# Fillers that move every large tile to a multiple of 512 bytes, and warm-up matmuls in float32r at several offsets

## The chip, the cores and the metric

The kernel runs on one core of a Trainium2 chip. The metric is the device time of one execution in microseconds (us); lower is better. Profiled times count from the start of the span, which is the time from the first to the last instruction.

## The reference

One decoder block on x of 512 positions by 1024 channels, all in float32:

```python
p = x @ w_in + b_in                        # 1024 -> 7184 columns
a_u, a_v, q, k, v, r, a_low, g_a, g_b = split(p)
y_a = gelu(a_u) * (causal_W_s @ layer_norm(gelu(a_v)) + b_s)      # 128-position chunks, 8 groups
log_f = log_sigmoid(a_low @ w_gate2 + b_gate) / 16
o = gated_linear_attention(q, k, v, log_f)                        # 4 heads, chunked
y_b = rms_norm(o) * norm_g * silu(r)
m = sigmoid(g_a) * y_a + sigmoid(g_b) * y_b
h = layer_norm(alpha * x + m @ w_out)
out = layer_norm(alpha * h + relu(h @ w_ff1)**2 @ w_ff2)          # 1024 -> 4096 -> 1024
```

## The kernel before, in words

**Three passes for one product.** Each operand of a large product is split into a float32r part "hi" (a cast on ScalarE, L90) and a remainder "lo" (a subtraction on VectorE, L91). A product is then three float32r matmuls: hi by hi, hi by lo, lo by hi. Activations stand in `xh`/`xl` (later `mh`/`ml` for m, `oh`/`ol` for combinations of the hidden layer, `Fs` and again `xh`/`xl` at the end); weights are streamed from HBM in chunks of 128 x 1024 (`raw`) and split into `wh`/`wl`, in rings of seven tiles each.

**Groups of 24.** Nearly all of TensorE's work is in groups of 24 matmuls, eight (or twice four) slices of the contraction by three passes, into one PSUM tile of 128 x 512. Which operand is stationary (loaded as 128 columns) and which one moves (512 columns) differs by line:

- L271 `first`: weights stationary, `xh`/`xl` moving; 4 groups.
- L204 `ps`: a row product. The activation is stationary, the weights move; 16 groups with `xh`/`xl`, and 8 with `mh`/`ml` (the product with w_out).
- L608 `qk`, `u`, `ga`, `r`, `gb` (36 groups) and `f`, the hidden layer (28 groups): weights stationary, `xh`/`xl` moving. Four more blocks of `f` run as 8 groups with 256 moving columns.
- L898 `m`: the second feed-forward product in a scheme of seven products for eight; `oh`/`ol` stationary, the weights move; 21 groups, alternating with groups of `f`.
- L984 `f`: the last quarter of that product; `Fs` or `xh`/`xl` stationary, the weights move; 7 groups of 512 columns and 2 of 256.

That is 120 groups of 24 with 512 columns and 10 with 256. Smaller work (scores `sc` L478, `pm` L656, `po` L504 to L508, transposes) runs in plain float32, each matmul as two instructions. The order of TensorE's instructions is the order of the program; from the hidden layer on that holds for the other engines too, and before it a scheduler orders them.

**Warm-up.** At the start `WARM = 9` float32 matmuls of 128 x 128 on the constant tile `ones` (L238) run while x and the first weights arrive.

**Where tiles lie.** Pools are stacked from both ends of each partition's memory, `side="left"` from below and `side="right"` from above, and each tile's start is rounded up to 32 bytes. As the program is built, the small constants in front (`ident`, `ones`, `ones_r`, `cols_sb`, three scalars) end at byte 18400 of each partition, and the right side starts at byte 229344. Both are multiples of 512 plus 480. Large tiles are multiples of 512 bytes long, so nearly all start there too:

| tiles | start, remainder by 512 |
|---|---|
| `xh`, `xl`, `wh`, `wl`, `als`, `dt`, `kt`, `bufA`, `bufB`, `raw`, `Fs` | 480 |
| `mh`, `ml`, `oh`, `ol` (behind the 896 bytes of statistics in pool `lnp`) | 352 |
| `ones_r` | 192 |
| `w2s`, `a_sb`, `wst` | 32 |
| `AT`, `QI`, `KD` of the first pair of heads; of the second | 480; 0 |

Slices of these tiles that go into a matmul begin at multiples of 512 bytes within the tile, so every stationary and every moving operand has the remainder of its tile.

Of the kernel before, what the change touches and what calls it, by code (L numbers as in the profile page):

```python
# [8 lines left out]
F32 = mybir.dt.float32  # L9
F32R = mybir.dt.float32r  # L10
# [5 lines left out]
P = 128  # L16
# [21 lines left out]
PAIRS = 3  # L38
ORDER = (2, 6, 3, 7, 4, 1, 5)
LEVELS = (32, 8, 2)  # L40
WARM = 9
QT_BUFS = 2
DIFF_K = "vector"
DIFF_Q = "gpsimd"
# [5 lines left out]
def hybrid_block(  # L50
# [20 lines left out]
    nc = tc.nc  # L71
    ctx.enter_context(tc.manual_schedule(engines={mybir.EngineType.PE}))

    def pool(stack, name, **kw):
        kw.setdefault("bufs", 1)
        return stack.enter_context(tc.tile_pool(name=name, reuse_waits="tile", **kw))

    const = pool(ctx, "const", side="left")
    xpool = pool(ctx, "xpool", side="left")
    wpool = pool(ctx, "wpool", side="left", bufs=W_BUFS)  # L80
    rpool = pool(ctx, "rpool", side="right", bufs=RAW_BUFS)
# [72 lines left out]
    ones = const.tile([P, P], F32, name="ones")  # L154
# [56 lines left out]
    def w_tile(u0, k, e):  # L211
        return [
            c.rearrange("p (k e) -> p k e", k=2)[:, k % 2, e * P : (e + 1) * P]
            for c in chunks[u0 + k // 2]
        ]
# [18 lines left out]
        nc.sync.dma_start(xraw[:, k0:k1, :], xT[:, k0:k1, :])  # L234

    wu = ps_a.tile([P, 512], F32, name="wu", tag="aux")
    for i in range(WARM):
        nc.tensor.matmul(wu[:, :P], ones, ones, start=True, stop=True)  # L238

    raw0 = rpool.tile([P, 1024], F32, name="raw0", tag="raw")  # L240
    raws[0] = [raw0]
# [9 lines left out]
    for k2 in range(KT // 2):  # L251
        split_to(k2 + 1)
        for k in (2 * k2, 2 * k2 + 1):
            wr = raw0[:, k * 512 : (k + 1) * 512] if k < 2 else None
            if k < 2:
                ksl = slice(k * 512, (k + 1) * 512)
                wh, wl = chunks[0]
# [10 lines left out]
            for i, e in order:  # L268
                wh, wl = w_tile(u0, k, e)
# [477 lines left out]
    lnp = pool(tail, "lnp", side="left")  # L747
    st1 = [lnp.tile([P, 2, 6], F32, name=f"st1_{t}") for t in range(NT)]
    st2 = [lnp.tile([P, 3, 6], F32, name=f"st2_{t}") for t in range(NT)]
    first_ln = ExitStack()  # L750
    ln1p = pool(first_ln, "ln1p", side="right")
    g1 = row_bcast(ln1p, ln1_g, D, "g1")
# [371 lines left out]
```

## Time and profile before

| | |
|---|---|
| median of three runs | 779.58 us (779.45 to 781.87) |
| profiled execution | 778.91 us, of which the span is 777.0 us |
| matmul instructions | 3498, busy 755.5 us |
| VectorE, ScalarE, GpSimd busy | 491.3, 355.7, 68.1 us |
| moved by DMA | 85.15 MB, mean 110 GB/s |

Busy time of TensorE is not its work at full rate: a matmul's record overlaps the next one's. What a group of matmuls costs is read from the time between the starts of successive groups.

### The profile page before, as it was taken

The page shows a single profiled execution, that of the slowest core. Times are in us where ns is not written, and L with a number is a line of the kernel's source. Part 1 is how long each engine was busy: PE and PEld are TensorE (multiplying, and loading weights), DVE is VectorE, ACT ScalarE, POOL GpSimd, SP SyncE. Part 2 cuts the span into 40 slices and gives each one's busy share as a digit, 9 for nine tenths or more (in the row PEclk, how much of TensorE's full clock was granted, in tenths as well). Part 3 has the DMA queues.
Part 4 walks back from the last instruction along what each step waited for, and adds up shares of the span by engine and source line. Part 5 has one row for each costly group of instructions (what it writes and reads, how often), then busy time and mean ns, then how long its engine had stood idle before and what let it go on. Part 6 is the DMA issues. An engine that isn't in the chain of part 4 may idle for free.

```text
span 777.0 us, 8849 instructions
## 1 busy us (share of the span) xinstructions
PE 755.5 (97%) x3498; PEld 627.2 (81%) x3498; DVE 491.3 (63%) x584; ACT 355.7 (46%) x453; POOL 68.1 (9%) x87
## 2 busy tenths in 40 slices
PE   8998999989999989999999999999999999999996
PEld 6887788878888877888888987888888888888785
DVE  6569666658666532445447545774687568869955
ACT  5476864353246544454322444555554444454300
POOL 1015400004202211000001000000000000000011
PEclk9999999999999999999999999999999999999999
DMA  7723332200341231422232522444154414335111
GB/s 274 262 74 116 102 129 81 82 28 27 109 136 55 74 130 36 151 85 93 97 101 76 163 82 83 159 136 138 54 162 136 147 69 145 130 132 163 54 55 54
DMA packets 25609, 85.15 MB, mean 110 GB/s; under 512 B 3104, under 2 KB 3360, under 8 KB 25568
## 3 DMA queue, kind: packets, MB, share of 16 engines
q1 hardware_dynamic: 25568, 84.59, 32.9%
q8 instruction: 27, 0.44, 0.2%
q14 instruction: 14, 0.11, 0.1%
HBM read 82.48 MB, written 2.10 MB: 109 GB/s over the span
## 4 chain that ended last, share of the span: by engine, by line
PE 85%; DVE 6%; ACT 3%; issue 2%; DMA 1%; POOL 1%; SPq 0%; DVEq 0%; POOLq 0%
PE f L608 22%; PE m L898 14%; PE ps L204 13%; PE gb L608 6%; PE r L608 6%; PE f L984 5%; PE u L608 5%; PE ga L608 4%; PE qk L608 3%; PE first L271 2%; DVE wl L91 2%; PE sc L478 2%; DMA raw<-in_w_all 1%; ACT wh L90 1%; PE po L504 1%
## 5 line engine op out<-in xcount | busy, mean ns | idle before, releaser
L91 DVE TENSOR_TENSOR wl<-raw,wh 128x1024 fp32r<-128x1024 f32 x144 | 176.9, 1238 | 152.1 <-ACT wh L90 145.3
L90 ACT CAST wh<-raw 128x1024 fp32r<-128x1024 f32 x144 | 148.7, 1045 | 137.9 <-PE ps L204 34.4
L608 PE MATMUL f<-xh,wl 128*128 128x512 f32 (+1 forms) x288 | 105.5, 366 | 0.0
L608 PE MATMUL f<-xh,wh 128*128 128x512 f32 (+1 forms) x288 | 105.4, 366 | 0.0
L608 PE MATMUL f<-xl,wh 128*128 128x512 f32 (+1 forms) x288 | 105.4, 366 | 0.0
L898 PE MATMUL m<-wh,ol 128*128 128x512 f32 x168 | 66.4, 395 | 0.5 <-DVE ol L91 0.5
L898 PE MATMUL m<-wh,oh 128*128 128x512 f32 x168 | 66.6, 396 | 0.3 <-ACT oh L90 0.3
L898 PE MATMUL m<-wl,oh 128*128 128x512 f32 x168 | 66.3, 395 | 0.0
L608 PEld LDWEIGHTS f<-xh,wh 128*128 128x128 f32 x288 | 54.3, 189 | 9.0
L608 PEld LDWEIGHTS f<-xl,wh 128*128 128x128 f32 x288 | 54.3, 189 | 9.0
L608 PEld LDWEIGHTS f<-xh,wl 128*128 128x128 f32 x288 | 54.3, 189 | 8.8
L204 PE MATMUL ps<-wh,xh 128*128 128x512 f32 x128 | 50.8, 397 | 0.0
L204 PE MATMUL ps<-wh,xl 128*128 128x512 f32 x128 | 49.9, 390 | 0.0
L204 PE MATMUL ps<-wl,xh 128*128 128x512 f32 x128 | 49.8, 389 | 0.0
L827 ACT ACTIVATE F<-f 128x512 f32<-128x512 f32 (+1 forms) x28 | 15.0, 537 | 75.9 <-PE f L608 75.9
L124 DVE TENSOR_TENSOR raw<-raw,raw 128x1024 f32<-128x1024 f32 x30 | 36.7, 1222 | 7.2 <-DMA raw<-in_w_all 6.9
L419 POOL TENSOR_TENSOR qt<-cum 128x768 f32<-128x768 f32 (+2 forms) x18 | 30.2, 1707 | 115.8 <-DVE cum L374 102.3
L898 PEld LDWEIGHTS m<-wh,ol 128*128 128x128 f32 x168 | 31.6, 188 | 8.4 <-DVE ol L91 1.0
L898 PEld LDWEIGHTS m<-wh,oh 128*128 128x128 f32 x168 | 31.6, 188 | 8.0 <-ACT oh L90 0.7
L898 PEld LDWEIGHTS m<-wl,oh 128*128 128x128 f32 x168 | 31.7, 189 | 7.4
L991 POOL TENSOR_TENSOR rs_l<-rs_l,nhalf 128x1 f32<-128x1 f32 x4 | 3.9, 986 | 332.9 <-DVE rs_l L990 332.9
L90 ACT CAST oh<-d 128x1024 fp32r<-128x1024 f32 x15 | 15.8, 1051 | 37.4 <-DVE d L824 37.4
(226 smaller groups left out, 1520.8 us busy)
## 6 DMA issues: line engine op xcount, KB each, us to landing
raw<-in_w_all SPq DMA_DIRECT2D x139, 512.0 KB, 3.3
xr<-in_x SPq DMA_DIRECT2D x8, 256.0 KB, 4.1
out<-bufA SPq DMA_DIRECT2D x8, 256.0 KB, 2.0
bufA<-in_xT SPq DMA_DIRECT2D x3, 512.0 KB, 9.0
brow<-in_b_in SPq DMA_DIRECT2D x4, 256.0 KB, 5.7
g<-in_ln_g SPq DMA_DIRECT2D x2, 512.0 KB, 4.6
b<-in_ln_b SPq DMA_DIRECT2D x2, 512.0 KB, 5.4
bufA<-in_xT SPq DMA_DIRECT2D x2, 256.0 KB, 3.3
```

Of the source, the lines that this page charges most:

```text
L90: nc.scalar.copy(hi, src)
L91: nc.vector.tensor_tensor(lo, src, hi.bitcast(F32), op=ALU.subtract)
L124: nc.vector.tensor_tensor(raw, raw, other[0], op=ALU.add if STREAM[i][0] == "sum" else ALU.subtract)
L204: nc.tensor.matmul(ps, s_, m_, start=(k == 0 and i == 0), stop=(k == KT - 1 and i == 2))
L271: nc.tensor.matmul(first[e], s_, m_[:, k, :], start=(k == 0 and i == 0), stop=(k == KT - 1 and i == 2))
L419: getattr(nc, DIFF_Q).tensor_tensor(qv[:, :, s0 : s0 + n, :], c4[:, :, d:4, :], c4[:, :, 0:n, h - 1 : h].broadcast_to([P, na, n, h]), op=A ...
L478: nc.tensor.matmul(sc[:, c, 0:192], pr.kt[:, jc * P : (jc + 1) * P], pr.qt[:, jc, :], start=True, stop=True)
L504: nc.tensor.matmul(po, pr.AT[:, j, c, :], vs, start=True, stop=(c == 0))
L608: nc.tensor.matmul(ps, s_, m_, start=(k == 0 and i == 0), stop=(k == KT - 1 and i == 2))
L827: nc.scalar.activation(dst, ps, AF.Relu)
L898: nc.tensor.matmul(ps, s_, m_, start=(k == 0 and i == 0), stop=(k == 3 and i == 2))
L984: nc.tensor.matmul(ps, s_, m_, start=(f == 0 and i == 0), stop=(f == 7 and i == 2))
```

## The change

Three tiles that nobody reads are added: 32 bytes behind the left side's constants (`pad_l`), 480 bytes at the right end (`pad_r`), 128 bytes behind the statistics of pool `lnp` (`pad_n`). The left side's large tiles then start at 18432 = 36 x 512, the right side's stack at 228864 = 447 x 512, and `mh`, `ml`, `oh`, `ol` at a multiple of 512 as well. All tiles that stood at remainder 480 or 352 stand at 0; `ones_r` stays at 192; `w2s`, `a_sb`, `wst` go to 64, and the second pair's `AT`, `QI`, `KD` from 0 to 32.

The nine float32 warm-up matmuls of 128 columns become 15 float32r matmuls of 512 columns. They read a tile `idle`, which takes the first place in the ring `wh`, is set to ones by VectorE (768 columns), and is read as the moving operand from 128 + o columns on, with o = 0, 4, 8, 24 and 40 columns (0, 16, 32, 96 and 160 bytes).

```diff
-WARM = 9
+WARM = (0, 0, 4, 4, 4, 8, 8, 8, 24, 24, 24, 40, 40, 40, 0)
...
     const = pool(ctx, "const", side="left")
+    const.tile([P, 8], F32, name="pad_l")
+    pool(ctx, "end", side="right").tile([P, 120], F32, name="pad_r")
     xpool = pool(ctx, "xpool", side="left")
...
-    for i in range(WARM):
-        nc.tensor.matmul(wu[:, :P], ones, ones, start=True, stop=True)
+    idle = wpool.tile([P, 1024], F32R, name="idle", tag="wh")
+    nc.vector.memset(idle[:, 0:768].bitcast(F32), 1.0)
+    for o in WARM:
+        nc.tensor.matmul(wu, idle[:, 0:P], idle[:, P + o : P + 512 + o], start=True, stop=True)
...
     st2 = [lnp.tile([P, 3, 6], F32, name=f"st2_{t}") for t in range(NT)]
+    lnp.tile([P, 32], F32, name="pad_n")
```

## Rows read from the trace of the kernel before

**Rows 1.** The page: busy time by engine, granted clock by slice, ending chain by engine.

```profile
PE 755.5 (97%) x3498; PEld 627.2 (81%) x3498; DVE 491.3 (63%) x584; ACT 355.7 (46%) x453; POOL 68.1 (9%) x87
...
PEclk9999999999999999999999999999999999999999
...
PE 85%; DVE 6%; ACT 3%; issue 2%; DMA 1%; POOL 1%; SPq 0%; DVEq 0%; POOLq 0%
```

**Rows 2.** Waits of TensorE, first and last of 13: total us, times, longest.

```profile
PE po L504 <- DVE t L714: 3.1, 2, 2.0
...
PE po L504 <- ACT bufB L522: 0.3, 1, 0.3
```

**Rows 3.** Chain that ended last, in order of time: start us, us, what.

```profile
33.51 10.88 PE ps L204 x48
...
103.41 1.30 PE sc L478 x8
...
382.43 33.47 PE ps L204 x144
...
428.82 2.87 PE f L608 x24
...
493.27 5.59 PE m L898 x24
498.86 5.46 PE f L608 x24
504.32 5.59 PE m L898 x24
509.90 5.46 PE f L608 x24
```

**Rows 4.** TensorE's groups by form: count | busy us, mean ns of one.

```profile
L608 PE MATMUL f<-xh,wl 128*128 128x512 f32 x224 | 87.3, 390 | 0.0
...
L898 PE MATMUL m<-wh,oh 128*128 128x512 f32 x168 | 66.6, 396 | 0.3 <-ACT oh L90 0.3
```

**Rows 5.** Windows: length, busy PE, PEld, DVE, ACT, POOL, clock, DMA share.

```profile
382.00:424.00 42.00, 42.00 (x190) 34.23 (x189) 25.06 (x32) 8.62 (x11) 2.65 (x4) 1.00 0.29 94
...
488.00:493.00 5.00, 5.00 (x24) 4.11 (x23) 3.68 (x5) 1.70 (x3) 0.00 (x0) 1.00 0.34 114
493.00:498.00 5.00, 5.00 (x24) 4.03 (x23) 3.59 (x4) 3.63 (x5) 0.00 (x0) 1.00 0.32 104
```

**Rows 6.** Timeline of the opening: start us, us, engine, line, instruction.

```profile
1.07 4.21 PE L238 MATMUL wu<-ones 128*128 128x128 f32 x18 [1.07 <-POOL bal L290]
...
4.70 1.84 DVE L259 CAST wh<-raw 128x512 fp32r<-128x512 f32 x1 [4.70 <-DMA raw<-in_w_all]
...
6.69 1.17 PE L271 MATMUL first<-xh,wh 128*128 128x512 f32 x4 [1.41 <-DVE wh L259]
...
8.60 1.07 PE L271 MATMUL first<-xh,wl 128*128 128x512 f32 x4
...
17.60 0.91 DVE L283 MEMSET als<- 128x1024 f32 x1 [0.16 <-issue]
```

**Rows 7.** The same chain in its first 30 us.

```profile
3.12 8.19 DMA raw<-in_w_all
...
12.42 1.24 DVE wl L91
...
13.70 16.18 PE first L271 x70
```

**Rows 8.** Timeline of TensorE around 165 us.

```profile
163.97 0.63 PE L608 MATMUL qk<-xl,wh 128*128 128x512 f32 x1
164.40 0.63 PE L608 MATMUL qk<-xh,wl 128*128 128x512 f32 x1
...
166.48 0.40 PE L608 MATMUL qk<-xl,wh 128*128 128x512 f32 x1
166.71 0.40 PE L608 MATMUL qk<-xh,wl 128*128 128x512 f32 x1
```

## The prediction

> **What bounds the kernel now.** I read the page first: TensorE is busy for 97% of the span, at full granted clock in every slice, and has 85% of the chain that ended last; VectorE is at 63% and ScalarE at 46% [rows 1]. Then TensorE's waits: the longest in total is 3.1 us, the last of the 13 is 0.3 us [rows 2], and the page's own chain leaves only 15% of the time to everything else. So the time is set by how closely matmuls follow each other, and that is read from the chain in order of time, as the distance of successive groups [rows 3]. The reader should see three numbers in it. A group of 24 with remainder 480 for both operands takes 10.88 / 2 = 5.44 us (L204 with `xh`, 48 matmuls) or 5.46 us (L608 `f` between two groups of `m`): 227 ns for each matmul. A group of `m`, with its stationary operand at remainder 352, takes 5.59 us, 233 ns each, and so do the groups with `mh`/`ml`: 33.47 us for 144, 5.58 us for 24 [rows 3]. And 512 columns at 2.4 GHz need 213.3 ns, so the fast kind pays 13.4 ns and the slow kind 19.6 ns on top of every matmul.
>
> **What the distance depends on.** The extra of the fast kind is a fixed piece: 256 columns take 2.87 us / 24 = 119.6 ns, that is 106.7 + 12.9 [rows 3]. It is hidden when the array takes its columns more slowly: at half the clock two matmuls start 0.43 us apart, which is 512 / 1.2 = 427 ns and nothing more, and 0.23 us apart just after [rows 8]; and a float32 score matmul, whose 192 columns take 1.30 us / 8 = 162.5 ns, that is 384 cycles or 160 ns and 2.5 [rows 3]. I conclude that the extra lies on the reading side, which keeps up with the array at full clock with little to spare. The extra of the slow kind goes with the place of the stationary operand: L204 is slow with `mh` and fast with `xh`, with the same weights moving. It does not go with ScalarE's load, which differs between `m` and `f` (3.63 against 1.70 us in 5 us) but is low in the stretch of `mh` too (8.62 in 42 us, 1.0 in 5) [rows 5].
>
> **The fillers, part one: the slow groups.** With `pad_n`, `mh`, `ml`, `oh` and `ol` get the remainder of the weights that move past them, as `xh` has it now. There are 21 groups of `m` (504 matmuls; the rows show a third of them, 168, for one pass [rows 4]) and 8 with `mh`/`ml`. If the distance follows the remainder of the stationary operand relative to the moving one, they fall to 5.45 us, the middle of 5.44 and 5.46: 21 x (5.59 - 5.45) + 8 x (5.58 - 5.45) = 2.9 + 1.0 = 3.9 us. A lower bound is 0 (the place is not the cause); I take 3.9, because the same line shows both distances.
>
> **Part two: the 13.4 ns of every matmul.** No matmul of the trace with 512 float32r columns has its moving operand at remainder 0, so its price is bounded by rows. Above: 5.59 us for a group, the worst that a remainder does here. Below: the extra falls to the 2.5 ns of the score matmul, 215.8 ns or 5.18 us for a group. The nearest row is the one with both operands at one remainder, 5.44 to 5.46; after the change both still share one. I take no change of the 13.4 ns and keep both ends.
>
> **The warm-up.** Removed: 18 instructions of 4.21 us, from 1.07 to 5.28 us [rows 6]. Added: a memset of 768 columns on VectorE, 768 / 1024 x 0.91 = 0.68 us, on an engine whose first other work starts at 4.70 us [rows 6], so it costs nothing there; and 15 matmuls of 512 columns, at half clock 0.427 us each [rows 8]. If VectorE starts about when GpSimd's constants are made, they begin near 1.6 us and, if all are at half clock, end at 1.6 + 15 x 0.427 = 8.0 us; if the clock rises where it rose before (the first real matmuls, from 6.69 us on, are 0.23 us apart), some three of them are fast and they end near 7.4. The first real matmul starts at 6.69 us, so it is late by 0.7 to 1.3 us. What hides that: the chain of this stretch runs over the second chunk of weights (DMA to 11.31, `wl` from 12.42, TensorE goes on at 13.70) [rows 7]. Before 13.70 TensorE has 26 real matmuls, 26 x 0.227 = 5.9 us in a stretch of 7.0, so 1.1 us of lateness is absorbed. Cost: 0 to 0.2 us; I take 0. Uncovered, it would be the 1.3 us, and if the clock rose late enough for 12 real matmuls at 0.427, some 2.4 us more. `idle` takes one place in the ring of `wh`; seven tiles later `wh5` takes its place, and the warm-up is then long over, while `wh6` reuses the place of `wh0` as before. No transfer moves.
>
> **Rest.** The float32 matmuls change their places too, but they have the reading to spare (2.5 ns over their columns [rows 3]): 0. `ones_r` stays off by 192 for 16 matmuls: 0. VectorE and ScalarE keep their operations: 0. The stretch near 165 us, where the clock was at half for six to seven matmuls [rows 8], costs 6.5 x 0.2 = 1.3 us now; it hangs on a wait and may go or come again: plus or minus 1.3.
>
> **Sum.** 778.91 - 3.9 = 775.0 us for an execution like the profiled one. The median of the runs is 0.67 us above that one, so 775.7 us, with 772 to 778 as this case's own range.
>
> **The rivals.**
> *A. The 13.4 ns go too.* 32 columns of 4 bytes at 2.4 GHz are 13.3 ns, and remainder 480 is 32 bytes short of a boundary; a read that begins inside a 128-byte piece touches one piece more, for 256 columns as for 512, and a slower array hides it. All three fit. Against it: a fixed cost of each load of a stationary operand fits as well. Price: 91 groups x (5.45 - 5.18) + 29 x (5.59 - 5.18) + 10 x (2.87 - 24 x 0.1092) = 24.6 + 11.9 + 2.5 = 39 us at most; as 85% of the chain is TensorE's [rows 1], I count 33: 779.6 - 33 = 746 us (741 to 768, since part of the extra may stay). [...]
> *B. Nothing changes.* The slow groups are slow for another reason than the place, say the side on which the weights are written while they move; then 779.6 us, 777.4 to 782. For it: `m` and the `mh` groups are also late in the kernel. Against it: the `f` between the `m` are as late and take 5.46 us [rows 3]. [...]
> *C. Slower.* With every operand at the same boundary, the load of the next stationary operand and the moving stream, which start together, meet in the same place at every matmul, and all groups take what the worst take now: 91 x (5.59 - 5.45) + 10 x 0.06 = 13 us, 779.6 + 13 = 793 us at the worst. It decides from 5.45 + 3.9 / 91 = 5.49 us for a group of `f`; above that the kernel loses.
>
> **How the numbers follow.** The forecast (both kinds near 227) 0.42, A 0.28, B 0.14, C 0.16. A measurement tells a change from none beyond about 0.3%, 2.3 us. Faster: A and nearly nine tenths of the forecast, 0.28 + 0.37 = 0.65; same: 0.05 + 0.14 = 0.19; slower: 0.16. The range reaches down to A's 742 and up to 782, which takes in B and the mild end of C and leaves out about 0.17. The likeliest case gives 775.7.
>
> **What would show it.** In the changed kernel's chain, `m` at 5.45 us beside `f` at 5.45 shows part one; `f` near 5.2 shows A; `m` still at 5.59 shows B; `f` at 5.5 or more shows C. The warm-up is right if TensorE still goes on near 13.7 us after `wl`; it is wrong if real matmuls near 8 us are 0.43 us apart. Within the warm-up, matmuls at full clock whose distance changes with the offset would speak for A, equal ones for a fixed cost. The prediction fails if the 13.4 ns hang on the absolute start, in either direction.

## The result, and the profile after

The changed kernel takes 774.75 us (median of six runs, 774.03 to 776.27) against 779.52 us for the kernel before: a ratio of 0.994, 95% interval 0.992 to 0.996. That is 4.8 us or 0.6% less; 775.7 was predicted. Its profiled execution has a span of 772.9 us, 4.1 less than before; the other 0.7 lies within the spread of the kernel before, whose six runs go from 778.15 to 781.87 us.

The chain of the changed kernel that ended last, in order of time (start us, us, what), the lines that answer to [rows 3] and [rows 7]:

```profile
13.63 16.17 PE first L275 x70
...
163.35 7.08 PE qk L612 x24
...
382.31 32.67 PE ps L206 x144
...
427.71 2.87 PE f L612 x24
...
481.28 5.28 PE m L903 x22
...
492.00 5.44 PE m L903 x24
497.44 5.44 PE f L612 x24
...
704.16 10.89 PE f L612 x48
...
726.79 39.17 PE f L989 x194
```

and of the kernel before:

```profile
482.39 5.39 PE m L898 x22
...
708.58 10.59 PE f L608 x47
...
730.91 39.15 PE f L984 x194
```

A group of `m` fell from 5.59 to 5.44 us and the `mh` groups from 33.47 to 32.67 for six; the `f` between the `m` fell from 5.46 to 5.44. The groups that were fast stayed: 2.87 us for 256 columns, and the plain 512-column groups are 227 ns a matmul as before. When the same piece of work starts in both chains shows where the 4.1 us came from:

| the work that starts | before, us | after, us | ahead by |
|---|---|---|---|
| first matmuls behind the second chunk | 13.70 | 13.63 | 0.07 |
| first group with `mh` | 382.43 | 382.31 | 0.12 |
| first group of `f` | 428.82 | 427.71 | 1.11 |
| first group of `m` | 482.39 | 481.28 | 1.11 |
| last pair of `f` groups | 708.58 | 704.16 | 4.42 |
| the last quarter (L984, now L989) | 730.91 | 726.79 | 4.12 |
| end of the span | 777.0 | 772.9 | 4.1 |

So the eight `mh` groups gave 0.99 us, `m` and the `f` between them 3.31, and 0.30 were given back in front of the last quarter, where TensorE waits for splits on VectorE that had not become faster. The stretch at half clock near 165 us is there again (granted clock 0.50 from 163.5 to 166.5 us): 24 matmuls of `qk` take 7.08 us instead of 5.44.

The opening, from the timeline (start us, us, engine, line), beside [rows 6]:

```profile
1.02 0.70 DVE L240 MEMSET idle<- 128x768 f32 x1 [1.02 <-PEq L1118]
...
1.77 5.85 PE L242 MATMUL wu<-idle 128*128 128x512 f32 x15 [1.77 <-DVE idle L240]
...
7.46 1.09 PE L275 MATMUL first<-xh,wh 128*128 128x512 f32 x4
```

The first real matmul is 0.8 us later than before, and the chain behind the second chunk is not late for it.

One detail of the chapter on the change was put wrongly there: `pad_l` stands in front of the other constants, not behind them, so `ones_r` moves from 192 to 224. Only the 16 `sd` matmuls use it, eight of 512 and eight of 256 columns, and they keep their distances, 234 and 119 ns.

### The profile page after: what moved, and what is told of

It is laid out like the page before. It is cut to its first block, busy times and chain, and to the rows that moved or that the text cites. A ratio compares the mean times of both kernels' runs of the same rounds, so it can differ in the third digit from the quotient of the medians.

```text
span 772.9 us, 8847 instructions
## 1 busy us (share of the span) xinstructions
PE 752.5 (97%) x3495; PEld 627.1 (81%) x3495; DVE 490.8 (64%) x585; ACT 355.9 (46%) x453; POOL 68.5 (9%) x87
## 4 chain that ended last, share of the span: by engine, by line
PE 85%; DVE 7%; ACT 3%; issue 2%; DMA 1%; POOL 0%; SPq 0%; DVEq 0%; POOLq 0%
PE f L612 22%; PE m L903 14%; PE ps L206 13%; PE gb L612 6%; PE r L612 6%; PE f L989 5%; PE u L612 5%; PE ga L612 4%; PE qk L612 3%; PE first L275 2%; DVE wl L93 2%; PE sc L482 2%; DMA raw<-in_w_all 1%; ACT wh L92 1%; PE po L508 1%
## 5 line engine op out<-in xcount | busy, mean ns | idle before, releaser
L903 PE MATMUL m<-wh,ol 128*128 128x512 f32 x168 | 65.5, 390 | 0.5 <-DVE ol L93 0.5
L903 PE MATMUL m<-wh,oh 128*128 128x512 f32 x168 | 65.5, 390 | 0.3 <-ACT oh L92 0.3
L903 PE MATMUL m<-wl,oh 128*128 128x512 f32 x168 | 65.4, 389 | 0.0
L206 PE MATMUL ps<-wh,xh 128*128 128x512 f32 x128 | 50.8, 397 | 0.0
L206 PE MATMUL ps<-wh,xl 128*128 128x512 f32 x128 | 49.9, 390 | 0.0
L206 PE MATMUL ps<-wl,xh 128*128 128x512 f32 x128 | 49.8, 389 | 0.0
L903 PEld LDWEIGHTS m<-wh,ol 128*128 128x128 f32 x168 | 31.5, 188 | 7.5 <-DVE ol L93 1.0
L903 PEld LDWEIGHTS m<-wh,oh 128*128 128x128 f32 x168 | 31.5, 188 | 7.2 <-ACT oh L92 0.7
L903 PEld LDWEIGHTS m<-wl,oh 128*128 128x128 f32 x168 | 31.5, 188 | 6.6
```

What stands on the lines that cost most here:

```text
L206: nc.tensor.matmul(ps, s_, m_, start=(k == 0 and i == 0), stop=(k == KT - 1 and i == 2))
L903: nc.tensor.matmul(ps, s_, m_, start=(k == 0 and i == 0), stop=(k == 3 and i == 2))
```

## The experiments

**Only the filler behind the statistics.** Nothing else of the change is made: all operands then stand at 480.

```diff
     st2 = [lnp.tile([P, 3, 6], F32, name=f"st2_{t}") for t in range(NT)]   # the kernel before
+    lnp.tile([P, 32], F32, name="pad_n")
```

> The kernel before with one edit: the 128 bytes behind the statistics, so that mh, ml, oh, ol start at remainder 480 like all other operands; no filler at the ends, old warm-up. Theory R (the remainder of the stationary operand relative to the moving one decides): a group of m takes 5.44 to 5.46 us, mh 5.44, and the time is that of the changed kernel, about 775. Rival Q (starts at multiples of 512 bytes decide): m stays near 5.59 us and the time near 779.5.

775.33 us, ratio to the kernel before 0.9955 (0.9938 to 0.9971). Its chain:

```profile
491.58 5.44 PE m L899 x24
497.02 5.44 PE f L608 x24
```

The 128 bytes alone bring the gain, with every operand 32 bytes short of a multiple of 512. The multiples themselves are not what counts.

**All but the filler behind the statistics.**

```diff
-    lnp.tile([P, 32], F32, name="pad_n")   # the changed kernel
```

> The changed kernel without the 128 bytes behind the statistics: mh, ml, oh, ol at remainder 384 while the weights move from remainder 0, so 128 bytes apart, as in the kernel before. Theory R: m takes 5.59 us, mh 5.58, the groups of f between them 5.46, and the time is that of the kernel before, about 778.7 to 779.5. Rival Q (it is enough that the large weight tiles and xh, xl start at multiples of 512): m near 5.45 us and about 775.

778.34 us, ratio to the kernel before 0.9991 (0.9981 to 1.0). Its chain has the old distances, with `mh`, `oh` at remainder 384 and the weights at 0:

```profile
492.70 5.59 PE m L902 x24
498.29 5.46 PE f L612 x24
```

Theory R stands in both directions; the fillers at the two ends and the new warm-up bring nothing that can be measured: the interval of the ratio reaches 1.0.

**The old warm-up.**

```diff
-WARM = (0, 0, 4, 4, 4, 8, 8, 8, 24, 24, 24, 40, 40, 40, 0)   # the changed kernel
+WARM = 9
...
-    idle = wpool.tile([P, 1024], F32R, name="idle", tag="wh")
-    nc.vector.memset(idle[:, 0:768].bitcast(F32), 1.0)
-    for o in WARM:
-        nc.tensor.matmul(wu, idle[:, 0:P], idle[:, P + o : P + 512 + o], start=True, stop=True)
+    for i in range(WARM):
+        nc.tensor.matmul(wu[:, :P], ones, ones, start=True, stop=True)
```

> The changed kernel with the nine float32 warm-up matmuls of before. If the warm-up is neutral: 774.3 to 775.2, the first real matmul near 6.7 us instead of 7.2, and TensorE goes on after the second chunk's wl at 13.6 to 13.7 us in both. Rival W (the longer warm-up brings part of the gain by an earlier or steadier clock): slower than the changed kernel by 0.5 us or more, with real matmuls 0.43 us apart somewhere before 13 us. Rival W2 (it costs its lateness): faster by about 0.5.

774.50 us (774.28 to 775.53), which cannot be told from the changed kernel. The timeline and the chain:

```profile
5.10 1.62 PE L273 MATMUL first<-xh,wh 128*128 128x512 f32 x4
6.57 1.09 PE L273 MATMUL first<-xl,wh 128*128 128x512 f32 x4
...
13.25 16.16 PE first L273 x70
```

The first real matmuls start at 5.10 us, earlier than the 6.7 expected, in this run 0.37 us apart in the mean (four in 1.47 us, where full clock has 0.227 for one), which is the sign that rival W named; and yet the run is not slower, as TensorE goes on at 13.25, when the second chunk is split. That is before the 13.6 to 13.7 expected, as the chunk itself landed 0.4 us earlier in this run; when TensorE starts its first matmuls sets nothing. The warm-up is neutral.

**A scan of remainders.** In place of the 15 warm-up matmuls of the changed kernel stand 27 blocks of 30 matmuls on a tile of ones; each block has one line of its own:

```python
for _ in range(30):   # s, o in columns of 4 bytes
    nc.tensor.matmul(wu, idle[:, s : s + 128], idle[:, 384 + o : 896 + o], start=True, stop=True)
```

> The changed kernel with 27 blocks of 30 matmuls each in place of the 15 warm-up matmuls (the rest as it is; the time has no meaning, it is longer by the blocks, some 180 us). Read from it: the distance of the last 24 of each block. Blocks 1 to 16: moving operand at remainder 0, stationary at 0, 32, 64 up to 480 bytes. Theory R: 227 ns at 0, more at some other remainders, about 233 at 384 (the case of the kernel before). Blocks 17 to 20: both operands at 32, 128, 256, 480: R expects 227 in each; rival Q expects a difference from remainder 0. Blocks 21 and 22: moving operand off by 16 and by 4 bytes: 227 if nothing finer than 32 bytes counts. Blocks 23 and 24: 64 and 32 stationary columns instead of 128: if the 13.4 ns above 213.3 come from the load of the stationary operand (theory L), they fall to some 7 and 3 ns; if they belong to the moving float32r stream alone (theory S), they stay. Blocks 25 and 26: 256 and 128 moving columns: 120 and about 67 under S; at 128 the load itself may bind. Block 27: the same in bfloat16: near 216 if half the bytes per column take the extra away.

The timeline; a block's distance is the start of the next block less its own, over 30. That takes in the change to the next block: it gives 118 ns for the 128 moving columns of L270, whose own matmuls stand 112 apart.

```profile
7.74 6.97 PE L245 MATMUL wu<-idle 128*128 128x512 f32 x30
14.55 7.15 PE L246 MATMUL wu<-idle 128*128 128x512 f32 x30
21.55 7.16 PE L247 MATMUL wu<-idle 128*128 128x512 f32 x30
...
139.64 7.00 PE L264 MATMUL wu<-idle 128*128 128x512 f32 x30
146.47 7.11 PE L265 MATMUL wu<-idle 128*128 128x512 f32 x30
153.43 7.25 PE L266 MATMUL wu<-idle 128*128 128x512 f32 x30
160.51 7.06 PE L267 MATMUL wu<-idle 128*64 128x512 f32 x30
167.41 7.11 PE L268 MATMUL wu<-idle 128*32 128x512 f32 x30
174.36 3.75 PE L269 MATMUL wu<-idle 128*128 128x256 f32 x30
...
181.48 6.42 PE L271 MATMUL wu<-idle 128*128 128x512 bf16 x29
```

Mean distance of the matmuls within a block, from the starts in the trace:

| stationary off by (bytes), moving at 0 | ns |
|---|---|
| 0, 256 | 227 |
| 192, 448 | 229 |
| 32, 64, 96, 128, 160, 224 and the same plus 256 | 233 to 234 |
| both at 32, at 128, at 256, at 480 | 227 |
| moving off by 16 bytes; by 4, stationary at 0 | 232; 237 |
| 64 stationary columns; 32 | 230; 232 |
| 256 moving columns; 128 | 120; 112 |
| bfloat16 | 216 |

For starts at multiples of 32 bytes, the distance of the two operands decides, with a period of 256 bytes; where both stand does not. That is theory R, and it refutes the reason behind my rival A: at remainder 0 as at 480 the plain read takes 227 ns. The expectation that nothing finer than 32 bytes counts failed: a moving operand 16 or 4 bytes off costs 5 or 10 ns. Theory L fails as well: a quarter of the stationary columns does not shrink the 13.4 ns. With 128 moving columns the distance is 112 ns, where theory S wanted 67; what sets the pace there, no run shows.

**The period in the kernel.** `pad_n` of 384 bytes puts `mh`, `ml`, `oh`, `ol` at remainder 256.

```diff
-    lnp.tile([P, 32], F32, name="pad_n")
+    lnp.tile([P, 96], F32, name="pad_n")
```

> The changed kernel with 384 bytes behind the statistics in place of 128, so that mh, ml, oh, ol start at remainder 256 and the weights at 0. Theory P (only the distance by 256 bytes counts, as in the scan): m at 5.44 us, mh at 5.44 to 5.49, and the time of the changed kernel, 774.3 to 775.3. Rival Q (it has to be a multiple of 512): m above 5.5 and 777 or more.

774.88 us, ratio to the kernel before 0.994 (0.9924 to 0.9957), and the chain has

```profile
492.28 5.44 PE m L903 x24
```

Theory P holds.

**Finer places, and one column read again and again.** 26 blocks of 40 in the same manner; the last six are

```python
one, many = idle[:, 0:1].broadcast_to([P, 128]), idle[:, 384:385].broadcast_to([P, 512])
nc.tensor.matmul(wu, one, idle[:, 384:896])            # stationary: one column 128 times
nc.tensor.matmul(wu, idle[:, 0:128], many)             # moving: one column 512 times
nc.tensor.matmul(wu, one, many)
nc.tensor.matmul(wu[:1], idle[:, 0:1], idle[:, 384:896])
nc.tensor.matmul(wu[:, :384], idle[:, 0:128], idle[:, 384:768])
nc.tensor.matmul(wu, idle[:, 0:128], idle[:, 384:896].rearrange("p (a b) -> p b a", a=2))
```

> The changed kernel with 26 blocks of 40 matmuls in place of the warm-up (the time has no meaning). Blocks 1 to 20: moving operand at remainder 0, stationary off by 4, 8, 12, 16, 24, 48, 80, 112, 144, 176, 184, 188, 192, 196, 200, 208, 216, 240, 248, 252 bytes. The first scan had 227 ns at 0 and 256, 229 at 192 and 233 elsewhere. Theory F (227 is the floor, a fixed 16 cycles of 1.2 GHz that no placement removes): nothing under 226. Rival G (some finer place avoids the extra): one or more near 216, which would be worth some 30 us to the kernel. Blocks 21 to 23: the stationary operand one column read 128 times, the moving one one column read 512 times, and both. If the two reads meet in the memory (theory L), 216 in at least the blocks 22 and 23, since the moving stream then asks for one address; if the extra belongs to the float32r stream itself (theory S), 227 or more in all three. Block 24: one stationary column instead of 128: L expects 213 to 220, S 227. Block 25: 384 moving columns: 173.3, that is 160 and 13.3. Block 26: the moving columns taken from two halves in turn: no theory has a number; slower if neighbouring columns share a read.

```profile
184.40 9.24 PE L263 MATMUL wu<-idle 128*128 128x512 f32 x40
193.48 9.32 PE L264 MATMUL wu<-idle 128*128 128x512 f32 x40
202.63 8.91 PE L265 MATMUL wu<-idle 128*128 128x512 f32 x40
211.38 8.91 PE L266 MATMUL wu<-idle 128*128 128x512 f32 x40
220.12 9.33 PE L267 MATMUL wu<-idle 128*1 128x512 f32 x40
229.29 7.10 PE L268 MATMUL wu<-idle 128*128 128x384 f32 x40
236.23 8.79 PE L269 MATMUL wu<-idle 128*128 128x512 f32 x40
244.86 1.09 PE L301 MATMUL first<-xh,wh 128*128 128x512 f32 x4
```

The 20 finer places take 227 ns (252 bytes, line L263) to 233 ns, none less, as theory F wanted; that the 13.4 ns are cycles of a clock of 1.2 GHz, as it put it, no run shows. They also limit theory R. A stationary operand 252 bytes off has the same distance by 256 from the moving one as a moving operand 4 bytes off, and the two take 227 and 237 ns; 240 bytes and a moving operand 16 bytes off make such a pair too, with 228 and 232. So for starts this fine the distance by 256 does not decide alone; whether the place of the moving operand counts too, no block tells. Theories L and S both fail in part: a stationary operand of one address still costs 9.15 / 40 = 229 ns and a single stationary column 9.17 / 40 = 229, where L wanted 220 at most, while a moving operand of one address costs 8.75 / 40 = 219, where S wanted 227. So 8 of the 13.4 ns go with what the moving operand reads. 384 columns take 173.3 ns, which again is 160 + 13.3. For the last block no theory had a number, and it is the surprise: with its columns taken from two halves in turn, the same matmul takes 8.63 / 40 = 215.8 ns.

**Which order of columns.** 18 blocks of 40 with `turned(ap, a, c)`, c neighbouring columns from each of a parts in turn:

```python
def turned(ap, a_, c_):
    return ap.rearrange("p (a b c) -> p b a c", a=a_, c=c_) if c_ > 1 else ap.rearrange("p (a b) -> p b a", a=a_)
```

> The changed kernel with 18 blocks of 40 matmuls in place of the warm-up (the time has no meaning). Block 26 of the scan before, in which the moving columns come from two halves in turn, took 215.8 ns instead of 227. Block 1 repeats it. Blocks 2 and 3: two neighbouring columns from each half in turn, without and with the same order in the output; 4 to 8: 4, 8, 16, 64, 128 columns from each half in turn, output in the same order; 9: one column from each of four quarters; 10 and 11: as 4 and 7 with the output in order; 12: a two-dimensional pattern that comes to the same addresses as a plain read; 13: block 1 with the stationary operand 128 bytes off; 14: 256 columns from two halves; 15: every second column, 256 of them; 16: block 1 from an odd column; 17: plain read, output in another order; 18: plain read. Theory H (the extra comes from reading neighbouring columns one after the other, which share a piece of memory): 216 in 1 and 9, a rise towards 227 from block 2 to 8 with the length of the run, 109 in 14 and 15, 227 in 12, 17 and 18. Rival I (any pattern of two dimensions is read in another way): 216 in all of 1 to 13 but those that collapse to a plain read, whatever the run. Rival R: in 13 the 128 bytes cost some 6 ns here too; under H they cost nothing once the extra is gone.

```profile
8.06 8.79 PE L249 MATMUL wu<-idle 128*128 128x512 f32 x40
16.70 13.50 PE L250 MATMUL wu<-idle 128*128 128x512 f32 x40
30.02 13.51 PE L251 MATMUL wu<-idle 128*128 128x512 f32 x40
...
90.87 11.46 PE L257 MATMUL wu<-idle 128*128 128x512 f32 x40
102.17 10.16 PE L258 MATMUL wu<-idle 128*128 128x512 f32 x40
...
130.33 8.80 PE L261 MATMUL wu<-idle 128*128 128x512 f32 x40
138.96 4.63 PE L262 MATMUL wu<-idle 128*128 128x256 f32 x40
143.43 9.24 PE L263 MATMUL wu<-idle 128*128 128x256 f32 x40
```

| moving columns | ns |
|---|---|
| one from each half (stationary at 0; 128 bytes off; moving from an odd column) | 215.8; 215.8; 217.0 |
| runs of 2, 4, 8, 16, 64, 128 from each half | 333, 250, 243, 240, 227, 227 |
| one from each of four quarters | 283 |
| 256 columns from two halves; every second column, 256 of them | 111.8; 226.7 |
| plain, also with another order in the output | 226.7 |

Block 1 repeats and, at 215.8, is no slower with the stationary operand 128 bytes off, so rival R fails for this order. But theory H falls as a theory: it wanted 216 for the four quarters (283), a smooth rise with the run (333 for runs of two), and 109 for every second column (226.7: 256 columns so spread take as long as 512 in a row). Rival I falls too, since of the two-dimensional patterns only single columns from two halves beat the plain read. What stands is the one fact.

**The weights read in turn.** In the changed kernel, the weights that move (L206, L903, L989) are laid out in HBM so that reading two halves in turn gives the old order; the matmuls and their results are the same. In the expectations from here on, "theory H" stands for its number alone, 5.18 us for a group; its reason fell in the scan.

```diff
+    def in_turn(ap, c0=0, c1=None):
+        return ap.rearrange("p (a b) -> p b a", a=2)[:, c0 // 2 : c1 and c1 // 2, :]
...
-    enumerate(passes(hi[:, k, tsl], lo[:, k, tsl], wh, wl))                       # L903; L206, L989 alike
+    enumerate(passes(hi[:, k, tsl], lo[:, k, tsl], in_turn(wh), in_turn(wl)))
...
+    def in_halves(w):                                                             # layout of the weights
+        return w.reshape(-1, P, 2, 256, 2).transpose(0, 1, 2, 4, 3).reshape(-1, P, 1024)
```

> The changed kernel with the moving weights of L206, L903 and L989 stored so that two halves of 256 columns are read in turn (the order in memory is set when the arrays are laid out; the products are the same). That is 52 groups of 24 (24 row products, 21 of m, 7 at the end). Theory H (the 11 ns above 215.8 are the price of reading neighbouring columns one after the other): those groups fall from 5.44 to 5.18 us, 52 x 0.26 = 13.5 us, of which I count 85 to 100%: 761 to 763 us. Rival K (in the kernel other engines' traffic keeps the extra, or VectorE and ScalarE become the bound): above 768.

764.94 us, ratio to the kernel before 0.981 (0.980 to 0.983). The chain:

```profile
88.72 1.54 PE sc L485 x8
...
163.24 8.02 PE qk L615 x24
...
488.56 5.18 PE m L906 x24
493.74 5.46 PE f L615 x24
```

Theory H's number for the group is right; the time is 2 us above its range, with 9.8 us gained on the changed kernel where 13.5 were counted. The two chains, compared piece by piece, show where the rest went:

- Some 1.7 us in front of 90 us. Eight of the row products run there, but the scores (`sc`) behind them need `kt` from VectorE, which is ready at 88.6 us instead of 88.9, so TensorE is only 0.4 us ahead there, not 2.1.
- Some 1.2 us near 165 us. More of this stretch runs at half clock (granted clock 0.84 from 150 to 172 us, against 0.92 in the changed kernel), and the 24 matmuls of `qk` take 8.02 us instead of 7.08.
- Some 0.6 us among the groups of `m`: the `f` between them, whose operands are read as before, are back at 5.46 us.
- Some 0.5 us in front of the last quarter, where TensorE waits for splits on VectorE.

The `kt` in question, from VectorE's timeline:

```profile
87.35 1.23 DVE L439 TENSOR_TENSOR kt<-kt,k 128x1024 f32<-128x1024 f32 x1 [0.88 <-ACT kt L437]
```

The clock is also lower between 60 and 80 us (0.91 against 1.00), but this costs nothing that can be seen: the scores start 0.14 us behind the end of `kt`, as they do in the changed kernel (0.15). Two of the runs, at 764.0 and 764.65 us, had a mean granted clock of 0.995, nearly that of the changed kernel, and are above the range too. More than half of what is lost goes to waits that a faster TensorE does not shorten.

**Everything read in turn.** `xh` and `xl` too; their results stand in PSUM in another order and are read from there with a step of two columns.

```diff
-    enumerate(passes(wh[:, k, :], wl[:, k, :], ah[:, k, tsl], al[:, k, tsl]))
+    enumerate(passes(wh[:, k, :], wl[:, k, :], in_turn(ah[:, k, tsl]), in_turn(al[:, k, tsl])))
-        take(ps)
+        take(ps.rearrange("p (b a) -> p a b", a=2))   # with outputs viewed as "p (a b) -> p a b"
```

> As e8, and xh, xl are read in turn as the moving operand too (first, pa, qk, u, ga, r, gb and the hidden layer); their results then stand in PSUM in another order, and ScalarE and VectorE read them with a step of two columns. Theory H: all 120 groups at 5.18 us and those of 256 columns at 2.68 instead of 2.87: 120 x 0.26 + 2 = 33 us, counting 85%: 741 to 747 us. Rival K: the reads of PSUM with a step of two columns cost ScalarE or VectorE more than 0.2 us each (some 70 of them), or the splits of the weights (1.05 and 1.24 us for each chunk) no longer keep up; then 750 or more.

747.91 us (747.27 to 749.13), ratio to the kernel before 0.960 (0.9585 to 0.9613). That is 0.9 us above theory H's range and short of rival K's 750. The groups are at 5.18 us; the chain, a group of ScalarE that reads PSUM with the step (687 ns in the changed kernel), and TensorE's longest wait (2.1 us there):

```profile
370.74 31.27 PE ps L216 x144
...
470.73 5.18 PE f L622 x24
```

```profile
L635 ACT ACTIVATE bufA<-u,cols_sb 128x512 f32<-128x512 f32 x8 | 5.5, 685 | 0.0
```

```profile
PE sc L492 <- DVE qt L451: 3.9, 2, 3.2
```

Of 33 us at TensorE, 26.8 arrive (81%). The step costs ScalarE nothing in this group, 685 ns against 687. But VectorE and ScalarE no longer keep up everywhere: TensorE's waits add up to 20.0 us instead of 13.4, most of them for VectorE, and those 6.6 us are about what is missing.

**The same without the fillers.** The edits of the last two on the kernel before.

> As e9, on the kernel before: no fillers, old warm-up. Theory H, by the block of the scan in which 128 bytes of distance cost nothing once the columns are read in turn: the same time as e9 within 2 us, m at 5.18 us although its stationary operand is 128 bytes off. Rival R2 (the distance of the two operands costs its 6 ns here too): slower than e9 by 3 to 5 us, m at 5.3 or more.

747.90 us (746.44 to 749.83), ratio 0.960 (0.958 to 0.962). `m` is at 5.18 us with its stationary operand 128 bytes off:

```profile
488.77 5.18 PE m L908 x24
```

Read in turn, the moving operand leaves the fillers nothing to mend. This version takes 4.0% less than the kernel before, as the one with fillers does, and 3.5% less than the changed kernel.

## Why the prediction was right

**Part one** was right in mechanism and nearly in size. `mh`: 1.0 us predicted, 0.99 measured. `m`: 2.9 predicted; `m` and the `f` between them gave 3.31, since the group fell to 5.44 and not 5.45, and each `f` lost 0.02 us that the sum had not counted. Both ends of its bound were tried: without `pad_n` the gain is gone, with `pad_n` alone it is whole. The 0.4 us too little for `m` and `f` and the 0.3 given back to splits, which the sum did not have, nearly cancel.

**Part two** was right to leave the 13.4 ns as they are, and for the reason given: both operands shared a remainder before and after. Rival A had the price nearly right and the cause wrong. The extra is no boundary that the first read misses, for it is 227 ns at remainder 0, 32, 128, 256 and 480 alike; but it can be removed by the order of the columns, from 779.25 to 747.91 us, 31 of the 33 us that A counted. Nor does any run show reads that go by pieces of 128 bytes, as A supposed. That the reading side has little to spare at full clock fits two rows, bfloat16 with 216 ns and one repeated address with 219, but no run shows what in the reading takes the time. The lower end that was kept, 215.8 ns from the score matmul's 2.5, is what bfloat16 and columns read in turn take; float32r columns read in their order stay at 226.7.

**The rest of the sum.** The memset of 0.70 us (0.68 predicted) and a first real matmul at 7.46 (7.4 to 8.0) cost nothing behind 13.63, as argued. The warm-up itself settles nothing about offsets, as nine of its 14 distances were 0.427 us whatever the offset, the same as at granted clock 0.50 near 165 us. That the stretch near 165 us hangs on a wait is not settled: TensorE waited 1.04 and 1.30 us in front of it in the changed kernel, but 2.1 us for `qt` near 68 us, where the clock stayed at 1.00. Rival B fell with the first experiment, rival C with the `f` groups at 5.44: equal remainders are the fast case and not the slow one.

**What stays open.** Why unequal remainders cost up to 7 ns, why a moving operand 4 bytes off costs 10, why two halves in turn are read faster than neighbours, why runs of two are the worst of the orders tried, and whether another distance between the halves would do as well. No block tried halves at distances other than 1024 bytes (512 for 256 columns), so 216 may not hold for others.

## What to carry to other kernels

Read the distance between the starts of successive groups, for each line, and compare it with the columns over the array's rate, 2.4 a ns at full clock in these runs: here 5.59, 5.44 and 5.18 us for 24 matmuls were three places and orders of the same operands, hidden behind a busy share of 97%. For float32r, let stationary and moving operands start at one remainder by 256 bytes, which one small filler does (5.44 instead of 5.59 us for a group of `m`); or let the moving columns be read from two halves in turn, which was worth 4% here and made a distance of 128 bytes cost nothing. Then look again at what TensorE waits for: part of the gain goes to engines that did not get faster. When a measured distance and its explanation fit several mechanisms, a block of 30 matmuls for each variant inside the kernel's own opening tells them apart in one run.

## What the runs showed of the hardware

- At granted clock 0.50, float32r matmuls of 512 columns start every 426.7 ns, 1.2 columns a ns; at granted clock 1.00 the step from 256 to 512 columns costs 107.1 ns, 2.4 columns a ns.
- A float32r matmul of 512 columns at full clock starts every 226.7 ns when read in order, 256 every 119.6, 384 every 173.3: columns / 2.4 + 12.9 to 13.4 ns. bfloat16: 215.8.
- If the stationary operand starts at another remainder by 256 bytes than the moving one, the mean distance is up to 7 ns more (234 at 96 bytes in the scan), and the distances can repeat in a short cycle: in the kernel before, a group of `m`, 128 bytes off, repeats one of seven distances from 228 to 241 ns. 192 bytes cost only 2 and 252 bytes nothing, while a moving operand 4 bytes off costs 10.
- Moving columns taken from two halves in turn: 215.8 ns, with the stationary operand 0 or 128 bytes off. Runs of two from each half: 333; of four: 250; four quarters: 283.
- A read of PSUM with a step of two columns cost ScalarE nothing: 685 ns against 687 for 128 x 512.
